# Modulation passes of the first layer: rows of silu(c) in their own slots, loaded by halves, and passes issued at a set rate into the neighbourhood attention

## The chip, the cores and the metric

The kernel runs on one core of a Trainium2 chip. The metric is device time in microseconds of one execution. Before the change it is 1731.88 us, the median of three runs (1730.83, 1731.88 and 1736.24).

The engines are PE (TensorE; PEld is its weight load), DVE (VectorE), ACT (ScalarE), POOL (GpSimd) and SP (SyncE, which here only issues DMAs). Each takes its instructions in order.

## The reference, cut to what matters

One step of a two-layer trunk over 512 latent and 128 context tokens of width 1024, all in float32. Each layer has a modulated norm, a mixer and a gated convolutional feed-forward network. The modulation of a layer is six vectors of width 1024, for two conditioning vectors, `c` (latent tokens) and `c_ctx` (context tokens):

```python
mod = (jax.nn.silu(cvec) @ w + bias).reshape(-1, 1, 6 * D_MODEL)
sh1, sc1, g1, sh2, sc2, g2 = jnp.split(mod, 6, axis=-1)
h = rms_norm(x, norm_mix_g) * (1.0 + sc1) + sh1
x = x + g1 * mixer(h)
x = x + g2 * conv_ffn(rms_norm(x, norm_ffn_g) * (1.0 + sc2) + sh2)
```

The first layer's mixer has two head groups side by side: neighbourhood attention (eight heads, an 8x16 window of the grid and all context keys) and a bidirectional gated linear attention (GLA, four heads, decays from a low-rank gate). The second layer's mixer is grouped-query attention.

## The kernel before, in words

Tokens lie along the free dimension (640 columns, in two halves of 320), features along the partitions. Weights come by SP's DMAs in tiles of 512 KB (`ws`), and ACT and DVE (in the first layer's mixer every second time POOL) split them into a rounded and a remaining part (`wh`, `wl`, lines 111 and 112). A product takes three matmuls for each block of 128 features (line 153).

Stages, each with a pool of its own: `begin` (first norm and modulation), `mix0` (the first layer's mixer, `layer0`, to about 450 us), `ffn0`, `mix1`, `ffn1`.

**The modulation.** Two vectors of the first layer (0 and 1) are made by matmuls in `begin`. The other ten are made on DVE by `modulations` (line 298). `crow` holds `c` and `c_ctx` in a row; a DMA spreads 512 values of it over all partitions and ACT takes the silu (lines 305, 306). Then, for each vector, `ada_wt` gives eight blocks of 128 output features by 1024 inputs, in halves of 512. A step of the generator loads one half block (256 KB, `wa`, three buffers, line 313) and makes two passes over it, for the two conditioning vectors: a product with the row that also sums along the row (line 316, 128x512, with an accumulator read that follows it). So a vector takes 16 steps and 32 passes. The mixer makes vectors 2 to 4 of the first layer (48 steps); `ffn0` makes the other seven (112 steps, one after each evacuation of a product).

**The order.** The framework lists the instructions of each engine by priority in a simulated schedule; priority follows the order in which the program issues them, except where `high_priority` moves a block ahead. `issue_after(x)` holds the instructions of a block that are on the engine of `x` behind `x` in that engine's order; it says nothing of other engines.

**The first layer's mixer.** `layer0` makes keys and queries of the GLA, the low-rank gate, then a class `Fill` holds generators of products (`queue`: value, output-gate, and query and key projections of the attention, some 208 steps of matmuls) that other code draws from by `fill.some(n)`. Its list `aside` holds the generator of the modulation. One step of it is drawn before the gates (line 672). The gates (lines 724 to 747) are four passes over matmul, minimum, Abs, Exp, Ln and a scan along the tokens. Then follow pieces in the order `a0 s0 a1 o0 q0 s1 o1`:

- `a` (`gla_scores`): seven levels of decayed scores; each level makes two factors on DVE (lines 840 to 843, 847), ACT (Exp) and POOL (line 846), and small matmuls (line 860); six level blocks are masked (line 865). At each of six places two steps of the modulation are drawn (`SLEV`), at one more four (`SOFF`).
- `s` (`gla_states`): states of the GLA. Before it, `fill.some(0, 99)` draws all steps that are left.
- `o` (`gla_out`): its outputs. `q` puts the attention's first query and key projection ahead in the filling.

Then comes the neighbourhood attention: 20 units (for each of four head pairs two pairs of query blocks with two heads each, and one context unit) in a software pipeline of stages scores, exps, gather, values, norm and turn, whose `high_priority(offset=AHEAD)` puts them 300 places ahead. Between stages `fill.some(RNA)` draws 1.8 steps of filling. DVE adds the bias (line 1062), takes the maximum (1023) and normalises (1037); PE transposes (1070) and multiplies by the values (1089). The tiles with the transposed weights have the tag `napx` (four buffers), and the four rows of silu(c) in `mix0` use these same buffers.

## Time and profile before

| what | value |
|---|---|
| median of three runs | 1731.88 us |
| profiled execution, its own time | 1732.08 us |
| its span, first to last instruction | 1730.3 us |
| mean granted TensorE clock | 0.97 |
| busy PE, DVE, ACT, POOL | 1640.0, 1280.7, 720.9, 206.5 us |
| chain that ended last | PE 78%, DVE 15%, DMA 3%, ACT 2%, issue 2% |
| matmuls of line 153 in that chain | 66% of the span |
| L316 passes, all 320 in the run | 120.4 + 113.2 us |

"Busy" is time with an instruction running. PE's is pipelined, so full busy time is not its peak rate. The chain is followed back from the last instruction, at each step to what released it. In a group of instructions, "idle before" is the time the engine stood still just before them and what ended it. The granted clock is a share of 2.4 GHz; the other level is 1.2 GHz.

### The profile page before, as it was taken

The page shows a single profiled execution, that of the slowest core. Times are in us where ns is not written, and L with a number is a line of the kernel's source. Part 1 is how long each engine was busy: PE and PEld are TensorE (multiplying, and loading weights), DVE is VectorE, ACT ScalarE, POOL GpSimd, SP SyncE. Part 2 cuts the span into 40 slices and gives each one's busy share as a digit, 9 for nine tenths or more (in the row PEclk, how much of TensorE's full clock was granted, in tenths as well). Part 3 has the DMA queues.
Part 4 walks back from the last instruction along what each step waited for, and adds up shares of the span by engine and source line. Part 5 has one row for each costly group of instructions (what it writes and reads, how often), then busy time and mean ns, then how long its engine had stood idle before and what let it go on. Part 6 is the DMA issues. An engine that isn't in the chain of part 4 may idle for free.

```text
span 1730.3 us, 33463 instructions
## 1 busy us (share of the span) xinstructions
PE 1640.0 (95%) x13142; PEld 1565.2 (90%) x13142; DVE 1280.7 (74%) x2877; ACT 720.9 (42%) x1599; POOL 206.5 (12%) x475
## 2 busy tenths in 40 slices
PE   7978798989999999999999999899999999999997
PEld 6867787878999999999998888789999999999997
DVE  5899955775899989996656987996776644663664
ACT  4443255453533313322335566665453322331342
POOL 2134441210200000000003310100100000000001
PEclk8988889999999999999998999999999999999998
DMA  8624323322255455444232200120222222222222
GB/s 317 204 86 133 108 90 97 101 88 92 81 165 164 152 165 183 151 149 128 70 122 87 68 20 13 42 63 20 80 66 82 74 74 73 74 69 91 72 66 71
DMA packets 68014, 175.22 MB, mean 101 GB/s; under 512 B 7920, under 2 KB 9744, under 8 KB 66832
## 3 DMA queue, kind: packets, MB, share of 16 engines
q1 hardware_dynamic: 67024, 171.48, 30.7%
q8 instruction: 103, 1.69, 0.4%
q0 software_dynamic: 832, 1.60, 0.3%
q14 instruction: 55, 0.45, 0.1%
HBM read 165.71 MB, written 7.34 MB: 100 GB/s over the span
## 4 chain that ended last, share of the span: by engine, by line
PE 78%; DVE 15%; DMA 3%; ACT 2%; issue 2%; SPq 0%; POOL 0%; ACTq 0%; DVEq 0%; POOLq 0%
PE mm L153 66%; DVE junk L316 2%; PE gpo L1297 2%; DVE wa L316 2%; PE gpt L1285 1%; DVE wl L112 1%; PE gs L1276 1%; DMA wa<-in_ada_wt_dram 1%; DVE mx L1023 1%; PE gs L1277 1%; PE napo L1089 1%; PE ss L410 1%; DVE eb L847 1%; DMA x<-in_xT_dram 0%; DVE q L613 0%
## 5 line engine op out<-in xcount | busy, mean ns | idle before, releaser
L153 PE MATMUL mm<-hh,wl 128*128 128x320 f32 x2080 | 652.6, 316 | 5.3 <-DVE x L488 1.9
L153 PE MATMUL mm<-hl,wh 128*128 128x320 f32 x2080 | 648.3, 312 | 0.6 <-DVE hl L456 0.6
L153 PE MATMUL mm<-hh,wh 128*128 128x320 f32 x2080 | 641.9, 312 | 0.0
L111 ACT CAST wh<-ws 128x512 fp32r<-128x512 f32 x376 | 228.8, 615 | 447.8 <-PE mm L153 420.5
L153 PEld LDWEIGHTS mm<-hh,wl 128*128 128x128 f32 x2080 | 394.5, 190 | 15.8 <-issue 5.5
L153 PEld LDWEIGHTS mm<-hl,wh 128*128 128x128 f32 x2080 | 395.2, 190 | 3.0 <-issue 1.2
L153 PEld LDWEIGHTS mm<-hh,wh 128*128 128x128 f32 x2080 | 393.4, 190 | 0.4
L112 DVE TENSOR_TENSOR wl<-ws,wh 128x512 fp32r<-128x512 f32 x348 | 242.2, 699 | 157.4 <-ACT wh L111 156.7
L153 PE MATMUL mm<-glo,wh 128*128 128x320 f32 x704 | 217.6, 310 | 0.0
L153 PE MATMUL mm<-ghi,wh 128*128 128x320 f32 x704 | 217.3, 310 | 0.0
L153 PE MATMUL mm<-ghi,wl 128*128 128x320 f32 x704 | 216.3, 310 | 0.0
L488 DVE SCALAR_TENSOR_TENSOR x<-mm,mod,x 128x192 f32<-128x192 f32 (+2 forms) x240 | 96.6, 435 | 84.1 <-PE mm L153 83.2
L153 PEld LDWEIGHTS mm<-ghi,wl 128*128 128x128 f32 x704 | 132.0, 188 | 0.9 <-issue 0.9
L153 PEld LDWEIGHTS mm<-glo,wh 128*128 128x128 f32 x704 | 132.6, 188 | 0.0
L153 PEld LDWEIGHTS mm<-ghi,wh 128*128 128x128 f32 x704 | 132.4, 188 | 0.1
L316 DVE SCALAR_TENSOR_TENSOR junk<-wa,sb 128x512 f32<-128x512 f32 x160 | 120.4, 757 | 9.4 <-DMA wa<-in_ada_wt_dram 7.0
L316 DVE SCALAR_TENSOR_TENSOR wa<-wa,sb 128x512 f32<-128x512 f32 x160 | 113.2, 714 | 0.2
L522 POOL MEMSET u<- 128x1 f32 x88 | 8.9, 102 | 767.2 <-DVE gate L515 432.5
L525 ACT COPY u<-mm 128x320 f32<-128x320 f32 x88 | 37.8, 431 | 87.6 <-PE mm L153 83.2
L1029 ACT ACTIVATE gp<-gs,mx,rq 128x640 f32<-128x640 f32 x64 | 56.9, 889 | 36.6 <-DVE mx L1025 27.9
L592 PE MATMUL tm<-wl,hh 128*128 128x256 f32 x200 | 61.3, 312 | 8.3 <-ACT v L601 4.0
L528 ACT COPY u<-mm 128x192 f32<-128x192 f32 x88 | 28.4, 322 | 78.8 <-PE mm L153 78.8
(302 smaller groups left out, 2452.7 us busy)
## 6 DMA issues: line engine op xcount, KB each, us to landing
ws<-in_wu_dram SPq DMA_DIRECT2D x88, 512.0 KB
wa<-in_ada_wt_dram SPq DMA_DIRECT2D x160, 256.0 KB
ws<-in_wd_dram SPq DMA_DIRECT2D x32, 448.0 KB
aw<-in_ada_w_dram SPq DMA_DIRECT2D x8, 1024.0 KB
ws<-in_w_ab_dram SPq DMA_DIRECT2D x16, 512.0 KB
ws<-in_wd_dram SPq DMA_DIRECT2D x16, 512.0 KB
x<-in_xT_dram SPq DMA_DIRECT2D x16, 320.0 KB
ws<-in_w_gqa_dram SPq DMA_DIRECT2D x10, 512.0 KB
```

The costliest lines, as they stand in the source:

```text
L111: nc.scalar.copy(hi, src)
L112: eng.tensor_tensor(lo, src, hi, ALU.subtract)
L153: nc.tensor.matmul(ps, x, y[:, s], start=st, stop=sp_)
L316: nc.vector.scalar_tensor_tensor(w if v else junk, w, 1.0, cs[v, j], ALU.mult, ALU.mult, accum_out=acc[:, k, v, j:j + 1])
L410: nc.tensor.matmul(ps[0:rows, c:c + 2], part[:, t], onesd, start=True, stop=True)
L488: nc.vector.scalar_tensor_tensor(x[:, b:e], ps[:, b - HN * h:e - HN * h], gate[:, v, m:m + 1], old[:, b:e], ALU.mult, ALU.add)
L525: nc.scalar.copy(u[:, 1:321], ps)
L528: nc.scalar.copy(u[:, 321:513], ps[:, 0:192])
L592: nc.tensor.matmul(ps, hh[:, s], wlo, start=(k == 0), stop=False)
L847: nc.vector.tensor_tensor(eb[:, 0:NT], eb[:, 0:NT], q[:, 0:NT], ALU.mult)
L1029: nc.scalar.activation(dst, src, AF.Exp, bias=mx[:, i:i + 1], accum_out=sm[:, i:i + 1], **kw)
L1297: last = nc.tensor.matmul(po[64 * f:64 * f + 64, 0:128], vs[t][:, 64 * kv:64 * kv + 64], mates[f]["x"][:, 128 * t:128 * t + 128], start=(t ...
```

## The change: what it does

`Fill.some` loses its second argument. It has a rate, `pace`, in steps of the modulation for each call: 0 to the end of the gates, 0.9 (`PACEG`) in the pieces of the GLA, 0.4 (`PACEN`) in the attention. `beside` draws the steps; each step's DVE instructions are held behind `anchor`, the DVE instruction last noted by the surrounding code (the scans, the mask products, a state's copy, the normalisation). `until` and `all` draw only filling. What is left at the last head pair of the attention is drawn there at once.

`modulations` takes groups of vectors and keeps one half (two rows) of silu(c) at a time. In a group it makes all first halves and then all second halves, or the other way round, beginning with the half that is there. The mixer has the groups (vector 2) and (vectors 3, 4), hence three loads of a half; `ffn0` has seven groups of one vector, hence eight loads of a half, in four buffers. In the mixer the rows have two buffers of their own (tag `sb`). The constant `w2` of the gates moves into a buffer of the mixer, loaded by POOL's DMA queue in the mixer; `adarow` and `kx` move into the stages' pools. The output projection looks its gate `mod[0, 2]` up when it uses it.

```diff
-        def some(self, n, m=0):
-            while m and self.aside:
-                m -= 1
-                if next(self.aside[0], self) is self:
-                    self.aside.pop(0)
+        def beside(self, n):
+
+            while n and self.aside:
+                n -= 1
+                with ExitStack() as behind:
+                    if anchor[0] is not None:
+                        behind.enter_context(tc.issue_after(anchor[0].ins))
+                    if next(self.aside[0], self) is self:
+                        self.aside.pop(0)
+
+        def some(self, n):
+            self.due += self.pace
+            self.beside(int(self.due))
+            self.due -= int(self.due)
+            self.queued(n)
+
+        def queued(self, n):
             self.owed += n
...
     def modulations(todo, room):
 
 
-        cs = {}
-        for v in range(2):
-            for j in range(2):
-                cs[v, j] = b = room()[:, 0:512]
+        cs, at = [], None
+
+        def rows(j):
+            for v in range(2):
+                b = room()[:, 0:512]
                 nc.sync.dma_start(b, a["crow"][:, D * v + 512 * j:D * v + 512 * j + 512].to_broadcast([P, 512]))
                 nc.scalar.activation(b, b, AF.Silu)
...
+        for group in todo:
+            accs = {lg: sp.tile([P, KD, 2, 2], F32, tag="adacc", name="adacc", bufs=3) for lg in group}
+            for j in ((0, 1) if at in (None, 0) else (1, 0)):
+                if j != at:
+                    cs, at = list(rows(j)), j
+                for l, g in group:
+                    n = VECTORS.index((l, g))
+                    for k in range(KD):
+                        w = T("wa", "wa", n=512, bufs=NWA)
+                        nc.sync.dma_start(w, a["ada_wt"][n, k, :, 512 * j:512 * j + 512])
+                        junk = N("junk")[:, 0:512]
+                        for v in range(2):
+                            nc.vector.scalar_tensor_tensor(w if v else junk, w, 1.0, cs[v], ALU.mult, ALU.mult, accum_out=accs[l, g][:, k, v, j:j + 1])
+                        yield
...
-        side = modulations(todo, lambda: T("sb", "sb", n=512, bufs=4)) if todo else iter(())
+        side = modulations([[lg] for lg in todo], lambda: T("sb", "sb", n=512, bufs=4)) if todo else iter(())
...
+        w2 = C("w2")[0:64, 0:512].rearrange("p (d n) -> p d n", d=2)
+        nc.gpsimd.dma_start(w2, a["w2"])
...
-        side = modulations(VECTORS[0:3], lambda: T("sb", "napx", n=512, bufs=4))
+        side = modulations((VECTORS[0:1], VECTORS[1:3]), lambda: T("sb", "sb", n=512, bufs=2))
...
+        fill.pace = PACEG
...
                     fill.until(g_vg)
-                    fill.some(0, 99)
...
+        fill.pace = PACEN
...
-            xs, proj = [], OutProjection(a["w_abo"], 4, mod[0, 2])
+            xs, proj = [], OutProjection(a["w_abo"], 4, lambda: mod[0, 2])
...
+                        fill.beside(999)
                         fill.until(g_late)
...
-            fill.some(RLEV, SLEV)
+            fill.some(RLEV)
...
-        fill.some(ROFF, SOFF)
+        fill.some(ROFF)
...
-SLEV = 2
-SOFF = 4
+PACEG = 0.9
+PACEN = 0.4
```

## Rows read from the trace of the kernel before

**Rows 1.** The page, part 2: busy tenths in 40 equal slices of 43.3 us, one digit a slice, of PE and of DVE.

```profile
PE   7978798989999999999999999899999999999997
DVE  5899955775899989996656987996776644663664
```

**Rows 2.** Windows by stage: begin:end and length, then busy us (and instructions) of each engine, the mean granted TensorE clock as a share of 2.4 GHz, the DMA engines' busy share and GB/s. The first seven windows lie in the first layer, the last one in the second layer's attention.

```profile
54.00:112.00 58.00, 52.32 (x421) 48.46 (x420) 55.22 (x130) 25.06 (x48) 9.71 (x6) 0.94 0.54 178
112.00:222.00 110.00, 84.03 (x1469) 78.23 (x1468) 109.87 (x224) 35.02 (x64) 53.03 (x35) 0.86 0.31 103
222.00:245.00 23.00, 23.00 (x251) 20.97 (x251) 10.14 (x19) 11.78 (x20) 12.35 (x10) 0.83 0.24 76
...
273.00:355.00 82.00, 76.73 (x657) 66.04 (x657) 59.65 (x123) 44.03 (x116) 18.61 (x20) 1.00 0.29 87
355.00:392.00 37.00, 31.12 (x234) 27.05 (x231) 25.47 (x54) 19.45 (x53) 4.77 (x6) 0.91 0.27 87
392.00:460.00 68.00, 65.59 (x447) 60.97 (x446) 44.18 (x107) 28.72 (x56) 7.58 (x27) 0.97 0.29 90
460.00:800.00 340.00, 339.42 (x2315) 339.16 (x2314) 323.00 (x797) 114.49 (x257) 10.19 (x106) 1.00 0.50 158
980.00:1160.00 180.00, 163.50 (x1635) 146.25 (x1635) 157.82 (x441) 116.30 (x277) 20.26 (x14) 0.99 0.13 41
```

**Rows 3.** The same view for two of these windows, of the instructions of line 316 (the modulation passes) alone: DVE busy us and records. Each pass leaves two records, the pass and the read of its accumulator.

```profile
54.00:112.00 58.00, 33.62 (x94) 0.94 0.54 178
112.00:222.00 110.00, 46.19 (x98) 0.86 0.31 103
```

**Rows 4.** The chain of waits, shares by line: first in 54 to 112 us, then in 112 to 222, then in 273 to 392.

```profile
by line: DMA wa<-in_ada_wt_dram 23.4%; DVE junk L316 22.6%; DVE wa L316 17.4%; issue 7.9%; DVE cum L743 6.7%; DVE wl L112 6.1%; DVE gmin L740 4.8%; DVE hl L456 3.3%; DVE cum L745 2.5%; DVE gmin L730 1.4%; DVE v L599 1.2%; DVE acc L865 0.8%;
...
by line: DVE junk L316 20.8%; DVE wa L316 18.1%; DVE eb L847 11.4%; issue 7.3%; DVE eb L843 6.6%; DVE ea L841 6.3%; DVE wl L112 5.4%; DVE ea L840 4.2%; DVE eb L842 4.1%; DVE acc L865 3.7%; DMA ws<-in_w_ab_dram 3.2%; DVE att L895 2.2%; DVE v
...
by line: PE mm L153 30.5%; PE napo L1089 10.0%; DMA bias<-in_na_bias_dram 6.0%; PE napt L1070 4.6%; PE nas L1058 4.1%; DVE hl L112 3.8%; issue 3.4%; DVE mx L1023 3.4%; PE nas L1059 3.1%; DVE kl L699 2.9%; PE grs L984 2.7%; ACT nap L1029 2.5
```

**Rows 5.** Instructions of the gates by source line: min/median/max duration in ns, first and last start in us, shapes.

```profile
L728 PE MATMUL gate<-lr,w x16: 429/429/533, 79.6 to 89.0; 64*128 64x320 f32 x16
...
L730 DVE TENSOR_SCALAR gmin<-gate,b x4: 874/880/882, 82.5 to 91.9; 128x640 f32<-128x640 f32 x4
...
L731 ACT ACTIVATE gabs<-gate,b x4: 775/794/796, 83.4 to 92.8; 128x640 f32<-128x640 f32 x4
...
L733 ACT ACTIVATE gabs<-gabs x4: 737/742/752, 85.5 to 93.7; 128x640 f32<-128x640 f32 x4
L733 ACT ACT_TABLE_LOAD  x1: 1283/1283/1283, 84.2 to 84.2; - x1
...
L740 DVE TENSOR_TENSOR gmin<-gmin,gabs x4: 814/822/825, 96.5 to 104.0; 128x640 f32<-128x640 f32 x4
...
L745 DVE TENSOR_TENSOR_SCAN cum<-gscan,gmin x2: 1478/1480/1482, 104.8 to 110.0; 128x640 f32<-128x640 f32 x2
```

**Rows 6.** Who waited for whom, PE in 112 to 222 us: total us, times, longest us.

```profile
PE lev L860 <- DVE eb L847: 14.2, 6, 5.2
```

**Rows 7.** Timeline around two places in the scores: start us, us, engine, line, operation. A start is the record's; the engine takes the next instruction a little before the last one's record ends.

```profile
119.79 2.22 POOL L112 TENSOR_TENSOR wl<-ws,wh 128x512 fp32r<-128x512 f32 x1 [2.29 <-ACT wh L111]
...
120.80 1.76 DVE L316 SCALAR_TENSOR_TENSOR junk<-wa,sb 128x512 f32<-128x512 f32 x1
...
121.97 1.98 POOL L846 TENSOR_TENSOR ea<-ea,kqg 128x640 f32<-128x640 f32 x1
...
122.49 2.01 DVE L316 SCALAR_TENSOR_TENSOR junk<-wa,sb 128x512 f32<-128x512 f32 x1
...
131.18 0.68 DVE L316 SCALAR_TENSOR_TENSOR wa<-wa,sb 128x512 f32<-128x512 f32 x1
...
131.80 0.68 DVE L316 SCALAR_TENSOR_TENSOR junk<-wa,sb 128x512 f32<-128x512 f32 x1
```

**Rows 8.** Groups of DVE instructions in 112 to 222 us: busy us, mean ns of one, idle before.

```profile
L847 DVE TENSOR_TENSOR eb<-eb,kqg 128x640 f32<-128x640 f32 x13 | 15.4, 1199 | 0.0
L843 DVE TENSOR_TENSOR eb<-cum 128x320 f32<-128x320 f32 x13 | 9.7, 743 | 0.0
...
L840 DVE TENSOR_TENSOR ea<-cum 128x320 f32<-128x320 f32 x14 | 6.7, 478 | 0.0
L865 DVE TENSOR_TENSOR acc<-lev,mask 128x160 f32<-128x160 f32 x22 | 6.0, 310 | 0.0
```

**Rows 9.** Timeline from 45 us: the loads of the rows of c, the first silu of them and the first pass; in brackets the engine's idle time before and what ended it.

```profile
46.17 1.75 SPq L305 DMA_DIRECT2D sb<-in_crow_dram  x4
...
49.47 0.63 ACT L306 ACTIVATE sb<-sb 128x512 f32<-128x512 f32 x1 [1.82 <-DMA sb<-in_crow_dram]
...
54.53 0.69 DVE L316 SCALAR_TENSOR_TENSOR junk<-wa,sb 128x512 f32<-128x512 f32 x1 [2.19 <-DMA sb<-in_crow_dram]
```

**Rows 10.** Who waited for whom, SP's DMA queue in 54 to 222 us: total us, times, longest us.

```profile
SPq L313 <- DVE wa L316: 89.3, 39, 10.4
```

**Rows 11.** The same for PE in 273 to 392 us.

```profile
PE napt L1070 <- DVE nap L1037: 1.5, 2, 1.1
```

**Rows 12.** By source line: the mask products of the scores, and the bias sums of the attention (columns as in Rows 5).

```profile
L865 DVE TENSOR_TENSOR acc<-lev,mask x24: 294/308/316, 111.4 to 221.5; 128x160 f32<-128x160 f32 x24
...
L1062 DVE TENSOR_TENSOR nas<-nas,bias x16: 683/700/700, 273.6 to 385.6; 128x512 f32<-128x512 f32 x16
```

More of the change, by code (lines that the diff above doesn't have):

```diff
@@ L237, in run @@
             pass
+    anchor = [None]
     class Fill:
@@ L243, in __init__ @@
             self.queue, self.aside, self.owed, self.after = [], [], 0.0, None
+            self.pace, self.due = 0, 0.0
         def add(self, gen):
@@ L269, in until @@
             while gen in self.queue:
-                self.some(1)
+                self.queued(1)
         def all(self):
             while self.queue:
-                self.some(1)
+                self.queued(1)
     mod = {}
@@ L286, in spread_modulation @@
             nc.tensor.matmul(ps[j:j + 32, 0:128 * n], siluc[:, r, :], w[:, 128 * n * r:128 * n * (r + 1)], start=(r < 4), stop=(r >= 4))
-        row = sp.tile([P, 256], F32, tag="adarow", name="adarow")[:, 0:128 * n]
+        row = T("adarow", "adarow", n=256, bufs=2)[:, 0:128 * n]
         nc.scalar.copy(row, ps[:, 0:128 * n])
@@ L298, in modulations @@
     def modulations(todo, room):
-        cs = {}
-        for v in range(2):
-            for j in range(2):
-                cs[v, j] = b = room()[:, 0:512]
+        cs, at = [], None
+        def rows(j):
+            for v in range(2):
+                b = room()[:, 0:512]
                 nc.sync.dma_start(b, a["crow"][:, D * v + 512 * j:D * v + 512 * j + 512].to_broadcast([P, 512]))
                 nc.scalar.activation(b, b, AF.Silu)
-        for l, g in todo:
-            n = VECTORS.index((l, g))
-            acc = sp.tile([P, KD, 2, 2], F32, tag="adacc", name="adacc", bufs=2)
-            for k in range(KD):
-                for j in range(2):
-                    w = T("wa", "wa", n=512, bufs=NWA)
-                    nc.sync.dma_start(w, a["ada_wt"][n, k, :, 512 * j:512 * j + 512])
-                    junk = N("junk")[:, 0:512]
-                    for v in range(2):
-                        nc.vector.scalar_tensor_tensor(w if v else junk, w, 1.0, cs[v, j], ALU.mult, ALU.mult, accum_out=acc[:, k, v, j:j + 1])
-                    yield
-            m = new_mod(l, g)
-            for v in range(2):
-                nc.vector.tensor_tensor(m[:, v, :], acc[:, :, v, 0], acc[:, :, v, 1], ALU.add)
-                nc.vector.tensor_tensor(m[:, v, :], m[:, v, :], adab[:, l, g, :], ALU.add)
@@ new lines, in rows @@
+                yield b
+        for group in todo:
[12 more added lines that the diff above has]
+                        yield
+            for l, g in group:
+                m, acc = new_mod(l, g), accs[l, g]
+                for v in range(2):
+                    nc.vector.tensor_tensor(m[:, v, :], acc[:, :, v, 0], acc[:, :, v, 1], ALU.add)
+                    nc.vector.tensor_tensor(m[:, v, :], m[:, v, :], adab[:, l, g, :], ALU.add)
@@ L702, in qk_done @@
             if h == 1:
-                kx = sp.tile([P, CTX], F32, tag="kx", name="kx")
+                kx = T("kx", "kx", n=CTX, bufs=2)
                 nc.scalar.copy(kx, ps[:, 192:320])
@@ L742, in layer0 @@
             if d == 0:
[L743 removed]
+                anchor[0] = nc.vector.tensor_tensor_scan(c, gscan, mins[key], 0.0, ALU.mult, ALU.add)
             else:
[L745 removed]
+                anchor[0] = nc.vector.tensor_tensor_scan(rev(c), gscan, rev(mins[key]), 0.0, ALU.mult, ALU.add)
             cum[key] = c
             fill.some(RG2)
+        fill.pace = PACEG
         with tc.issue_after(last.ins):
@@ L1036, in norm @@
                 w = u["p"][i] if n > 1 else u["p"][i][:, 0:NT]
-                nc.vector.tensor_scalar_mul(w, w, sm[:, i:i + 1])
+                anchor[0] = nc.vector.tensor_scalar_mul(w, w, sm[:, i:i + 1])
         u["exps"], u["norm"] = exps, norm
@@ L1158, in begin @@
             parts, srcs = self.half(self.first, outs)
-            return products(srcs, parts, lambda m, h, ps: residual(xs[m], ps, h, self.gate, m), (("mm", "mm"),), 512)
+            return products(srcs, parts, lambda m, h, ps: residual(xs[m], ps, h, self.gate(), m), (("mm", "mm"),), 512)
         def end(self, outs, xs, olds=None):
@@ L1165, in begin @@
                 run(products(srcs[0:KD - FIN], parts, done, ("ps", ("p1", "p1")), 512))
-            return into_norm(xs, self.gate, begin, srcs, parts, 512, olds)
+            return into_norm(xs, self.gate(), begin, srcs, parts, 512, olds)
     def layer1(xs, rs, mods):
@@ L1318, in layer1 @@
         run(project(1))
-        proj = OutProjection(a["w_gqao"], 0, mod[1, 2])
+        proj = OutProjection(a["w_gqao"], 0, lambda: mod[1, 2])
         ys = []
```

7 lines of the change are left out of this document (2 added, 5 removed).

## The prediction

> **What bounds the kernel now.** I began with the slices of the page: DVE stands at 8 or 9 tenths from 43 to 216 us while PE falls to 7 and 8 tenths, the weakest stretch of the run [rows 1]. The windows by stage say it sharply: from 112 to 222 us DVE is busy 109.87 of 110 us, PE 84.03 at a mean granted clock of 0.86; PE idles 26 us there [rows 2]. The reader should see the other side in the same table: from 460 to 800 us PE is busy 339.42 of 340, so time lost or won before 460 passes straight to the end.
>
> Third, how much of DVE is the modulation passes of line 316: 33.62 us in 54 to 112 (94 records, so 47 passes with their accumulator reads) and 46.19 us in 112 to 222 (98, so 49) [rows 3]. All 48 steps (3 vectors x 16 steps x 2 passes) are over by 222 us. Fourth, the chain: from 54 to 112 it runs through these passes (22.6% and 17.4%) and their loads (23.4%); from 112 to 222 again through them (20.8% and 18.1%) [rows 4]. So the first layer waits for passes whose results are needed only by the output projection and the feed-forward network. In the neighbourhood attention, 273 to 392 us, DVE has 34 us free (59.65 of 82 and 25.47 of 37) and PE is busy 107.85 of 119 [rows 2].
>
> **The change part by part.** What follows is the count of steps. One is drawn before the gates, unpinned. Then each filling call adds 0.9: seven in a0, two in s0, seven in a1, two each in o0, s1, o1, so 22 x 0.9 = 19.8, or 19 steps, 14 of them to the end of a1. The 28 others come at 0.4 a call, so within some 68 calls; five units make 28 calls and the stages lag by up to two units, so that is near the 14th of 20 units.
>
> *A, before the scores (54 to 112).* Of 23.5 steps one is left. What is late next is the gates' own chain. The first gate's matmuls start at 79.6 [rows 5]; two of 0.43 and the minimum of 0.88 end near 81.4. ACT then has four times 0.79 + 0.74, two table loads of 1.28 and the first Ln, priced like an Exp: 9.4, to 90.8. DVE has four differences of 0.82 and four scans of 1.48 left, 9.2, and about 2 us of splits and copies for the filling: 102, against 111.4 now (last scan from 110.0) [rows 5]. I take -9. Bounds: -4, if PE, busy 52.32 of 58, delivers the filling first; -13.6, the share of the loads in the chain alone (23.4% of 58).
>
> *B, scores and states (112 to 222).* Without the 46.19 us DVE holds 63.7. Back come 14 steps, 28 passes. A pass takes 0.615 us from start to start when POOL is quiet (131.18 to 131.80) and on average 46.19/49 = 0.943 here: 17.2 or 26.4 us, sum 80.9 or 90.1, so -29 or -20. PE's 84.03 then lies beside it; at a mean clock of 0.86 a part of it ran at 1.2 of the 2.4 GHz, so it is less at full clock. PE also waits 14.2 us for the second factor of the scores, behind passes on DVE [rows 6], and that shrinks. I take -18, the dearer pass and 2 us for two engines that must alternate. Bounds: -29 and -8.
>
> Why a pass is dear here: at 120.80 one takes 1.69 to the next start, while POOL's split of 119.79 runs to 122.0; the next, at 122.49, lasts 2.01 beside the product that POOL has from 121.97 to 123.95; at 131.18 and 131.80, POOL silent, 0.68 [rows 7]. Others are stretched alike: L843 has a mean of 743 ns where L840, of the same shape, has 478 [rows 8]. The Trainium skill, "SBUF — State Buffer", section "Who interferes with whom", says that a VectorE instruction with two SBUF inputs contends with a GpSimd one that reads SBUF, for the whole instruction, and that issue order decides who blocks. The trace agrees: L865, which has one input in PSUM, keeps 310 ns [rows 8]. By that rule POOL's work blocks whichever such DVE instruction is next, so the waiting is not taken away with the passes. That is a rival below.
>
> *C, 222 to 245.* PE is busy throughout at a clock of 0.83, a part of it at 1.2 GHz, after the idling before; at 2.4 throughout this is 23 x 0.17 = 3.9 us less. I take -2, ends -4 and 0: idle gaps remain.
>
> *D, rows of silu(c) by halves.* Three pairs of rows instead of two, in two slots of their own. Twice in this layer a new half is loaded when the old half's last pass is over: issue, landing, silu, pass. At the start this takes from 46.17 (issue) to 54.53 (first pass), 8.4 us for four rows, with ACT waiting 1.82 for the first landing [rows 9]. In SP's queue the other loads stand behind that issue, which waits for DVE; in ACT's queue two silu of 0.63 and up to two table loads of 1.28 stand before exponentials. Bounds: 0, if the neighbouring work fills the gap, and 16, two full latencies on the path. I take +3, nearer to the hidden end, since ACT has only 35 of 110 us to do in 112 to 222. The weight loads of the passes waited 89.3 us in SP's queue behind passes already [rows 10], so that queue is no new gate.
>
> *E, the neighbourhood attention.* 28 steps are 56 passes of 0.615, 34.4 us. With the 85.12 of 273 to 392 this is 119.5 of 119: no gap is left. The nearest row is the second layer's attention, by the same pipeline: 980 to 1160 with DVE at 157.82/180 = 0.877 and PE at 163.50/180 = 0.908 [rows 2]. At 0.877, 119.5 us need 136, +17. But the attention's stages go ahead in the order, so passes slip behind them, to where DVE has 24 of 68 us free (392 to 460): over 273 to 460, (129.3 + 34.4)/187 = 0.875, just what the second layer bears, +0. Bounds: 0, and +25, if all end with unit 14, near 355: (59.65 + 34.4)/0.877 = 107 for 82. Queued behind each pass on DVE are the bias sum, the maximum, the normalisation; PE waits for these little now (1.5 us for the normalisation) [rows 11]. I take +11, between 0 and 17 and nearer the second layer's crowding.
>
> *The rest.* The feed-forward network of the first layer gets 16 rows where it had 4: 12 x 0.63 = 7.6 us of ACT, busy 114.49 of 340; DVE, busy 323, gets nothing. I take 0, bounds 0 and +5. w2 comes by POOL's queue in the stage itself, before the gates at 79.6, with POOL busy 9.71 of 58: 0, up to +2. The other buffers that move change no instruction. The attention's buffers that held the rows were free by 222, well before its first unit near 273, so giving them back is worth 0.
>
> Sum: -9 -18 -2 +3 +11 = -15. The profiled execution took 1732.08 (span 1730.3, 1.8 around it), 0.2 above the median of 1731.88: 1717.
>
> **The rivals.**
> *More: the passes hide in the attention.* A -9, B -23, C -2, D and E 0: -34, 1698. For it: 58 us of DVE free between 273 and 460, enough for 34. Against it: the free time there is partly the chain's own waiting.
> *The waiting stays.* POOL blocks other two-input work in place of the passes. The waiting is 46.19 - 49 x 0.615 = 16 us; kept whole, 63.7 + 17.2 + 16 = 97 of 110, B = -13, sum -10: 1722. For it: L843 and, with a mean of 1199 ns, L847 are stretched as well [rows 8]. Against it: with DVE no longer full, some of the blocking falls on idle time. The page named under B states the rule behind this.
> *Slower: the attention pays for every pass.* Each pinned pass stands on the in-order DVE in front of a sum, a maximum or a normalisation on which PE's next transposes rest: all 34.4 us lie on the path. A, B, C and D give -26, so +8: 1740. It decides from an attention longer by 26 us. For it: DVE has no time left over in 119. Against it: PE has filling matmuls there (L153 holds 30.5% of the chain [rows 4]) and hardly waits for DVE now.
> *It doesn't do what it says.* The pin only holds a pass behind an instruction of DVE; nothing holds the rest of the scores in front. If the passes still end up in the gaps before the scores, each engine does as before: -2, 1730.
>
> **How the numbers follow.** A measurement tells about 0.3%, 5 us, from no change. Forecast 0.41, more 0.15, waiting stays 0.13, slower 0.19, as before 0.12. Of the forecast and the waiting together 0.06 falls within 0.3%, and of "as before" 0.08, with 0.03 faster and 0.01 slower: faster 0.66, same 0.14, slower 0.20. The bounds of all terms together go further than 1695 to 1740, but they don't fall together; this range takes in the first rival and the last and leaves about 2 in 10 out.
>
> **What would show it.** A right: the last scan ends near 102 and the chain before it has no loads of wa. B: the last L865, now at 221.5, comes near 195, with DVE under 97% busy before it and the clock over 0.86. E: the time from the first L1062 to the last, now 112 us [rows 12], is 5 to 17 us longer, with DVE near 0.9. D: ACT and DVE wait for the crow loads under 5 us in all. Wrong, if the scores don't end 15 us earlier, or if the attention grows by more than 26.

## The result: slower, 1754.34 us, and the profile after

The changed kernel takes 1754.34 us (median of four runs, 1752.76 to 1755.34) against 1731.36 for the kernel before beside it: ratio 1.0131, 95% interval 1.0118 to 1.0143. That is 23 us slower where 15 us faster was forecast. Its profiled span is 1751.0 us against 1730.3, the granted clock 0.963 against 0.970.

The gain forecast up to the end of the scores came, and was lost behind them. Starts in us from the two traces (before: [rows 5, 12] and the first line below):

| milestone | before | after | difference |
|---|---|---|---|
| last scan of the gates | 110.0 | 97.0 | -13.0 |
| last mask product of the scores | 221.5 | 197.1 | -24.4 |
| last copy of a GLA output | 261.1 | 245.1 | -16.0 |
| first bias sum of the attention | 273.6 | 275.9 | +2.3 |
| last bias sum of the attention | 385.6 | 406.9 | +21.3 |

By source line, the copies of the GLA outputs of before, then four milestones of after (count, then min/median/max ns, first and last start):

```profile
L958 ACT COPY got<-go x4: 570/586/587, 246.8 to 261.1; 128x512 f32<-128x512 f32 x4
...
L768 DVE TENSOR_TENSOR_SCAN cum<-gscan,gmin x2: 1478/1480/1481, 90.5 to 97.0; 128x640 f32<-128x640 f32 x2
...
L890 DVE TENSOR_TENSOR acc<-lev,mask x24: 306/311/324, 98.9 to 197.1; 128x160 f32<-128x160 f32 x24
...
L983 ACT COPY got<-go x4: 573/586/590, 226.3 to 245.1; 128x512 f32<-128x512 f32 x4
...
L1087 DVE TENSOR_TENSOR nas<-nas,bias x16: 678/690/700, 275.9 to 406.9; 128x512 f32<-128x512 f32 x16
```

The windows by stage of after (columns as in [rows 2]: PE, PEld, DVE, ACT, POOL busy, granted clock, DMA share, GB/s):

```profile
54.00:112.00 58.00, 52.48 (x445) 48.22 (x444) 37.78 (x53) 30.55 (x56) 20.09 (x11) 1.00 0.25 81
112.00:222.00 110.00, 98.50 (x1665) 89.06 (x1664) 93.60 (x184) 42.45 (x75) 56.33 (x39) 0.91 0.33 104
222.00:245.00 23.00, 19.00 (x140) 16.75 (x138) 9.65 (x24) 11.53 (x23) 7.07 (x7) 0.85 0.26 89
245.00:273.00 28.00, 12.30 (x90) 11.64 (x90) 8.30 (x20) 5.07 (x11) 3.87 (x6) 0.63 0.50 141
275.00:400.00 125.00, 104.77 (x769) 91.82 (x768) 112.58 (x270) 59.45 (x151) 22.84 (x25) 0.84 0.40 126
392.00:460.00 68.00, 67.36 (x479) 61.39 (x478) 38.49 (x81) 26.87 (x61) 1.84 (x13) 1.00 0.24 82
460.00:800.00 340.00, 338.55 (x2301) 336.28 (x2300) 324.09 (x793) 129.37 (x287) 16.66 (x121) 0.99 0.50 161
```

The first two lines are the success: DVE is no longer full (37.78 of 58 for 55.22, 93.60 of 110 for 109.87 [rows 2]) and PE does 98.50 us of work for 84.03. The fourth is a hole that was not there: PE stands 15.7 of 28 us. The fifth is the attention: DVE 0.90 busy, PE 104.77 of 125 at a clock of 0.84. Nothing changes after it: from the start of the last bias sum to the end of the span it takes 1344.7 us before and 1344.1 after. The kernel before in the same 125 us:

```profile
275.00:400.00 125.00, 113.79 (x927) 97.39 (x926) 87.33 (x184) 64.36 (x172) 23.38 (x26) 0.97 0.27 84
```

The hole in the timeline of after (start, us; in brackets idle before and what ended it):

```profile
239.58 4.76 SPq L807 DMA_DIRECT2D vc<-in_na_vc_dram  x1
...
244.44 1.25 SPq L811 DMA_DIRECT2D kc<-in_na_kc_dram  x2
...
245.74 4.09 SPq L333 DMA_DIRECT2D wa<-in_ada_wt_dram  x3
...
246.43 0.31 PE L152 MATMUL mm<-hh,wl 128*128 128x320 f32 x1
...
246.58 0.31 PE L152 MATMUL mm<-hl,wh 128*128 128x320 f32 x1
...
257.86 1.29 ACT L110 CAST kch<-kc 128x512 fp32r<-128x512 f32 x2 [9.41 <-DMA kc<-in_na_kc_dram]
259.31 0.69 DVE L336 SCALAR_TENSOR_TENSOR junk<-wa,sb 128x512 f32<-128x512 f32 x1 [10.95 <-DMA wa<-in_ada_wt_dram]
...
260.12 0.49 DVE L722 TENSOR_TENSOR kl<-mm,kk 64x320 fp32r<-64x320 f32 x1
...
260.76 0.61 PE L152 MATMUL mm<-hh,wl 128*128 128x320 f32 x1 [13.28 <-DVE kl L722]
...
261.96 0.47 PE L152 MATMUL mm<-hl,wh 128*128 128x320 f32 x1
...
262.23 0.47 PE L152 MATMUL mm<-hh,wh 128*128 128x320 f32 x1
```

Read it from the end. PE stands 13.28 us for the keys' split on DVE (L722). DVE has had that split's input since 248.04 + 0.42 (the ACT cast), but a pass (L336) is in front of it in DVE's order and waits 10.95 us for its weights. Those were issued at 245.74, behind the eight value tiles, `vc` and the cached keys, and are used 13.6 us later. Beside this wait stands a second one: ACT waits 9.41 us for the cached keys, issued at 244.44. After the hole PE restarts at the lower level: line 152 starts a matmul every 0.145 us at 246.4 (clock 1.00) and every 0.267 us at 262 (clock 0.50, 1.2 GHz).

The order in SP's queue is new as well. The value tiles (`vw`) and the cached keys (`kc`) in SP's timeline, before and then after:

```profile
237.60 0.90 SPq L787 DMA_DIRECT2D kc<-in_na_kc_dram  x2
...
251.83 13.55 SPq L781 DMA_DIRECT2D vw<-values  x8
```

```profile
228.13 11.35 SPq L805 DMA_DIRECT2D vw<-values  x8
...
244.44 1.25 SPq L811 DMA_DIRECT2D kc<-in_na_kc_dram  x2
```

The program issues these loads in the same order in both kernels; the framework's list put the keys 14 us ahead of the value tiles before the change and 16 us behind them after it. Which part of the change turned the order was not tried alone; e4 below, with the old draws and no pins, has the keys first (244.34 and 258.24), e1, without the steps of the attention, has them last.

### The profile page after: what moved, and what is told of

Read it like the earlier page. It is cut to its first block, busy times and chain, and to the rows that moved or that the text cites. A ratio compares the mean times of both kernels' runs of the same rounds, so it can differ in the third digit from the quotient of the medians.

```text
span 1751.0 us, 33552 instructions
## 1 busy us (share of the span) xinstructions
PE 1652.5 (94%) x13142; PEld 1575.5 (90%) x13142; DVE 1282.4 (73%) x2877; ACT 735.0 (42%) x1617; POOL 209.7 (12%) x475
## 4 chain that ended last, share of the span: by engine, by line
PE 72%; DVE 7%; ACT 1%; issue 1%; POOL 0%; DMA 0%; ACTq 0%; POOLq 0%; DVEq 0%
PE mm L152 63%; PE gpo L1322 2%; PE gpt L1310 1%; PE gs L1301 1%; PE gs L1302 1%; DVE mx L1048 1%; DVE wl L111 1%; PE napo L1114 1%; DVE wa L336 1%; PE ss L431 0%; DVE gp L1062 0%; DVE q L634 0%; PE napt L1095 0%; DVE junk L336 0%; DVE gkl L1253 0%
## 5 line engine op out<-in xcount | busy, mean ns | idle before, releaser
L152 PEld LDWEIGHTS mm<-hh,wl 128*128 128x128 f32 x2080 | 397.5, 191 | 33.8 <-issue 18.9
L336 DVE SCALAR_TENSOR_TENSOR junk<-wa,sb 128x512 f32<-128x512 f32 x160 | 114.7, 722 | 22.0 <-DMA wa<-in_ada_wt_dram 17.1
L336 DVE SCALAR_TENSOR_TENSOR wa<-wa,sb 128x512 f32<-128x512 f32 x160 | 116.9, 738 | 0.3
```

The costliest lines, as they stand in the source:

```text
L152: nc.tensor.matmul(ps, x, y[:, s], start=st, stop=sp_)
L336: nc.vector.scalar_tensor_tensor(w if v else junk, w, 1.0, cs[v], ALU.mult, ALU.mult, accum_out=accs[l, g][:, k, v, j:j + 1])
```

## The experiments

Times are medians, with the ratio and its 95% interval to the kernel before run beside them (1731 to 1732 us each time). "Change" is the changed kernel, 1754.34.

**e1: the change without the 28 steps of the attention.** Loads, passes and the rows' third load are left out; vectors 3 and 4 are summed in part.

```diff
+                        done[0] += 1
+                        if done[0] > limit:
+                            yield
+                            continue
                         w = T("wa", "wa", n=512, bufs=NWA)
...
-        side = modulations((VECTORS[0:1], VECTORS[1:3]), lambda: T("sb", "sb", n=512, bufs=2))
+        side = modulations((VECTORS[0:1], VECTORS[1:3]), lambda: T("sb", "sb", n=512, bufs=2), 20)
```

> The changed kernel with the last 28 steps of the first layer's modulation left out (their loads, passes and the third load of rows; the vectors 3 and 4 are then only partly summed); the 20 steps to the end of the GLA stay as they are. Theory of the queue plus theory of DVE time: all that the change loses comes after the GLA and from these 28 steps, so the gain at the GLA's end, 16 us (last copy of its outputs at 245.1 for 261.1), stays: about 1715. Rival, the new order itself (rows by halves, pins, keys behind the value tiles) costs the time: it stays above 1740.

1729.35, ratio 0.9984 [0.9969, 0.9998]: the steps cost 25 us, yet without them 2 us remain of a forecast gain of 29 (A, B and C), and of the 16 expected. Scores and GLA end as in the change (196.4, 246.7) and the attention is 112.8 us long, as before. Its first bias sum comes only at 267.9, and the chain of waits of e1 says why:

```profile
243.24 12.09 DMA kc<-in_na_kc_dram
```

With the pass gone, the second wait, for the cached keys, is on the path: 12.09 us.

**e2, e3, e5, e6: which wait holds the entry.** e2 lets the first ten calls of the attention draw no step; e3 moves the cached keys' loads ahead of the value tiles' loads in the program; e5 does both; e6 is e1 with e3's edit.

```diff
         def some(self, n):
-            self.due += self.pace
+            if self.skip:
+                self.skip -= 1
+            else:
+                self.due += self.pace
...
         fill.pace = PACEN
+        fill.skip, fill.due = 10, 0.0
```

```diff
+        for c in range(2):
+            kc, x, y = N("kc")[:, 0:512], C("kch", F32R)[:, 0:512], C("kcl", F32R)[:, 0:512]
+            nc.sync.dma_start(kc, a["na_kc"][:, 4 * c:4 * c + 4, :].rearrange("p h t -> p (h t)"))
...
         vw = {}
...
         nc.sync.dma_start(vc, a["na_vc"])
-        for c in range(2):
-            kc, x, y = N("kc")[:, 0:512], C("kch", F32R)[:, 0:512], C("kcl", F32R)[:, 0:512]
-            nc.sync.dma_start(kc, a["na_kc"][:, 4 * c:4 * c + 4, :].rearrange("p h t -> p (h t)"))
```

> The changed kernel, but the first ten filling calls of the attention draw no step (and nothing is owed from the GLA), so that the 21st step's load no longer stands between the value tiles' loads and the first unit. Theory of the queue: the stand of 13.3 us at 247 to 261 goes, at least down to what the wait of ACT for the cached keys leaves of it; 9 to 13 us faster than the change, 1741 to 1745. Theory of DVE time alone: the same 28 steps, a little closer together, so no faster than 1754. Rival of the keys: ACT waits for them until 257.9 anyway, so 3 us at most.

> The changed kernel with the two loads of cached keys issued before the value tiles' loads instead of behind them. Theory of the queue: DVE waits for the pass's own load (10.95 us), not for the keys, so within 3 us of the change, 1751 to 1757. Rival of the keys: ACT's wait of 9.4 us is what holds the stage, so about 9 us faster, 1745.

> Both edits together: the cached keys' loads ahead of the value tiles' loads, and no step for the first ten calls of the attention. Theory of two waits side by side (the first pass's load and the keys, both queued behind the value tiles, each enough to hold the stage): together they give what neither gives alone, 12 to 16 us faster than the change, 1738 to 1743. Rival, the stand has a third cause (the value tiles themselves, or PE's order): no more than the later start alone, 1747.

> The last 28 steps left out as in the first experiment, and the keys' loads ahead. The chain of the first experiment had 12.1 us of the keys' load on it; without it 8 to 12 us less than 1729: 1718 to 1721. The rival with a third cause: 1726 or more. The difference to the run with both edits is the price of the 28 steps in the attention: theory of DVE time 15 to 22 us; rival (the steps are hidden once nothing waits for loads): under 6.

e2: 1747.76 (1.0092 [1.0073, 1.0111]), -6.6, less than expected: its chain of waits has 13.12 us of the keys' load. e3: 1755.03 (1.0131 [1.011, 1.0152]), nothing. e5: 1745.89 (1.0078 [1.0062, 1.0093]), -8.4, less than expected. e6: 1723.01 (0.995 [0.9935, 0.9965]), 6.3 under e1.

The edit of the keys does less than the expectations say. SP's timeline of e6, and the longest piece of its chain of waits:

```profile
227.22 11.13 SPq L820 DMA_DIRECT2D vw<-values  x7
238.43 4.06 SPq L810 DMA_DIRECT2D kc<-in_na_kc_dram  x2
242.58 0.61 SPq L820 DMA_DIRECT2D vw<-values  x1
```

```profile
239.37 14.22 DMA kc<-in_na_kc_dram
```

Seven of the eight value tiles still go first (in e3, e5, e7 and e10 too; in e8 and e15 all eight). The keys are issued 4.2 us earlier than in e1 and land 1.7 us earlier (253.59 for 255.33), so the wait for them is shortened and not gone. e6's first bias sum is at 264.9, e1's at 267.9; where the rest of the 6.3 us comes from was not found. Two waits do stand side by side: shortening the keys' alone wins nothing, taking the pass away leaves the keys' (e1, e2). None of these four runs is without the second.

e5 and e6 differ in the 28 steps (and their third load of rows): 22.9 us. The attention is 130.7 us long in e5, 111.3 in e6. Their windows, e5 and then e6:

```profile
275.00:400.00 125.00, 105.02 (x752) 90.03 (x750) 111.98 (x277) 57.42 (x146) 21.91 (x24) 0.84 0.39 125
```

```profile
275.00:400.00 125.00, 114.51 (x921) 98.26 (x921) 84.90 (x188) 60.04 (x159) 22.42 (x37) 0.96 0.27 84
```

With the steps DVE has 27.1 us more in it, and PE pays twice: 9.5 us more idle, and the work it does is at a mean clock of 0.84, not 0.96. The passes lie on the path: in e5's chain of waits from 266 to 397 us they hold 21.3%, 28 us:

```profile
by line: PE mm L152 16.0%; DVE junk L339 10.7%; DVE wa L339 10.6%; DVE mx L1051 8.2%; issue 6.4%; DVE nap L1065 5.6%; DVE nas L1090 4.9%; DVE hl L111 4.0%; DVE kl L725 3.4%; DVE q L637 3.2%; DVE kk L726 3.0%; DVE wl L111 2.6%; DVE got L1013
```

**e11 to e14: pin, passes or loads.** All on e5. e11 holds no pass of the attention behind a normalisation. e12 keeps the 28 loads and leaves out the passes; e13 keeps both, but passes of 8 elements; e14 keeps full passes over one tile and leaves out the loads. In e12 to e14 vectors 3 and 4 are not the full sums.

```diff
-                    if anchor[0] is not None:
+                    if anchor[0] is not None and self.pace == PACEG:
```

```diff
-                        for v in range(2):
+                        done[0] += 1
+                        for v in range(2 if done[0] <= limit else 0):
```

```diff
+                        done[0] += 1
+                        e = 512 if done[0] <= limit else 8
                         for v in range(2):
-                            nc.vector.scalar_tensor_tensor(w if v else junk, w, 1.0, cs[v], ALU.mult, ALU.mult, accum_out=accs[l, g][:, k, v, j:j + 1])
+                            nc.vector.scalar_tensor_tensor((w if v else junk)[:, 0:e], w[:, 0:e], 1.0, cs[v][:, 0:e], ALU.mult, ALU.mult, accum_out=accs[l, g][:, k, v, j:j + 1])
```

```diff
+                        done[0] += 1
+                        if done[0] <= limit:
+                            w = T("wa", "wa", n=512, bufs=NWA)
+                            nc.sync.dma_start(w, a["ada_wt"][n, k, :, 512 * j:512 * j + 512])
...
```

> Keys first and later start, but the passes of the attention are not held behind a normalisation; in the pieces of the GLA they are held as in the change. Theory (DVE's time is what costs, wherever a pass stands): 1746 within 4, the attention 127 to 132 us long, DVE near 0.9. Rival (a pass costs since it is held in front of a sum or a maximum): the passes move into gaps of DVE, the attention is 118 to 122 us long, 1735 or less.

> Keys first and later start; the 28 steps of the attention issue their weight loads but not their 56 passes (so vectors 3 and 4 are summed in part only); the rows' third load stays. It splits the 22.9 us that the 28 steps cost into loads and passes. Theory (the passes' time on DVE costs): 1723 to 1726, the attention 111 to 114 us long. Rival (the loads in SP's queue or the DMA engines beside the bias and weight loads cost): 1732 or more, the attention over 119 us.

> Keys first and later start; the 28 steps of the attention keep their loads and both passes, held where they were, but a pass goes over 8 elements instead of 512 (vectors 3 and 4 are summed in part only). The loads come at the pace of the attention, which the run with the loads alone did not keep: without a reader they were all issued at its entry. If the passes' time on DVE is the price, 1723 to 1729, the attention 111 to 116 us long. If the loads are the price (SP's queue, where a load waits for the tile of three steps before, in front of the bias loads), 1738 to 1746, the attention over 122 us.

> The counterpart: keys first and later start, the 56 passes of the attention at their full width and place, all over the tile of the last step before, and none of the 28 loads (vectors 3 and 4 are wrong sums for it: their inputs are left out). If the passes' time on DVE is the price, 1740 to 1746, the attention over 124 us. If the loads are the price, 1723 to 1729, the attention 111 to 116 us long. Both prices may add up to more than the 22.9 us, if they overlap.

e11: 1750.02 (1.0109 [1.0092, 1.0126]), 4.1 over e5, and an attention of 136.5 us, longer than expected: the pin is not the price. e12: 1745.29 (1.0075 [1.0056, 1.0093]), a miss and a confounded one: with no reader the loads were issued at the entry, where the chain holds six of them in a row (261.72 to 284.5) in front of a bias load, so the first bias sum came at 277.7 instead of 266.1. e13: 1730.63 (1.0000 [0.9988, 1.0011]); e14: 1739.94 (1.0048 [1.003, 1.0065]). Over e6 that is 7.6 us for the loads at their pace and 16.9 for the passes, 24.5 together against 22.9. The 7.6 are not the loads alone: the short passes still take 9.05 us of DVE from 275 to 400, where e5's take 41.14. So the passes are two thirds of the price or more, the loads one third at most. The windows of e13 and then e14:

```profile
275.00:400.00 125.00, 112.03 (x893) 97.78 (x892) 91.15 (x296) 62.20 (x165) 21.77 (x25) 0.93 0.41 131
```

```profile
275.00:400.00 125.00, 103.50 (x812) 89.12 (x811) 113.97 (x285) 61.67 (x158) 23.12 (x25) 0.92 0.24 72
```

e14 has DVE and PE busy as e5 has them (113.97, 103.50) with the DMA share of 0.24, but a clock of 0.92 for 0.84 and 812 matmuls for 752; e13 has PE nearly as in e6. How e13's 7.6 us arise is not settled: the clock is 0.93, and in SP's queue the loads wait 32.0 us for passes (L345), 14 times, with bias and weight loads behind them.

**e4: halves and slots alone.** The buffers and halves of the change, with the old draws (two and four a place, all that are left before the states) and no pins.

```diff
-                    if anchor[0] is not None:
+                    if False:
...
-            fill.some(RLEV)
+            fill.beside(SLEV)
+            fill.some(RLEV)
...
                     fill.until(g_vg)
+                    fill.beside(99)
```

> Rows by halves in their own slots, w2 and the small buffers as in the change, but the steps drawn as before (2 at each level, 4 at the next place, all that are left before the states) and held behind nothing. Theories of the queue and of DVE time: these parts cost nothing, within 4 us of the kernel before, 1728 to 1736. Rival, the halves: three loads of rows with their silu and table loads cost 5 us or more, 1737 or above.

1738.98 (1.0045 [1.0029, 1.0061]): 7.6 us slower than before, as the rival had it. The last scan is at 98.2, but GLA's outputs end at 275.9 instead of 261.1. The passes come late: 16.93 us of them lie behind 222, where the kernel before has none, and DVE is busy 26.34 of the 28 us from there on. ACT waits 7.8 us for rows. That the halves alone make the passes late is argued: e4 holds all the moved buffers.

**e9, e16, e15, e17: SP's queue or the DMA engines.** e9 puts the keys first in the kernel before. e16 is the change with the value tiles and `vc` in POOL's queue. e15 draws all steps before the attention (8 before the gates, 1.8 a call in the GLA) with the keys first; e17 does so with the value tiles in POOL's queue instead.

```diff
-                nc.sync.dma_start(v, grid[4 * t:4 * t + 4, c0:c0 + 32, :])
+                nc.gpsimd.dma_start(v, grid[4 * t:4 * t + 4, c0:c0 + 32, :])
...
-        nc.sync.dma_start(vc, a["na_vc"])
+        nc.gpsimd.dma_start(vc, a["na_vc"])
```

```diff
-        next(side)
+        for _ in range(8):
+            next(side)
...
-PACEG = 0.9
+PACEG = 1.8
```

> The kernel before the change, with only the loads of the cached keys moved ahead of the value tiles' loads. Theory: the entry of the attention waits for this load with no pass about, as in the experiment without the 28 passes, where the same move gave 6.3 us; there the scores ended 25 us earlier. If the entry waits for it here too, 1725 (-6), with the first bias sum near 268 instead of 273.6. Rival: in the old order the last outputs of the GLA (261) are late enough that the keys are there in time; then 1731 within 2, and the first bias sum stays at 273 to 274.

> The change as it is, except that the eight value tiles and the cached values are loaded through POOL's queue instead of SP's; the order of everything else stays. If the entry of the attention stands still because the weights of its first modulation step and the cached keys lie behind these loads in SP's queue, both come early now: the first bias sum near 264 instead of 275.9 and 1742 to 1746. Rival: it is the DMA engines themselves that are taken, whatever the queue; then the loads land as late as before and 1752 to 1756 stays.

> Keys first, 8 steps before the gates, and twice the rate in the pieces of the GLA (1.8 a call for 0.9), so that all 48 steps are over before the attention; rows by halves as in the change. It keeps a part of the gain before the scores and pays nothing in the attention. Theory: the 39 steps in the GLA give 1.8 DVE us a step as they did before the change, so its outputs end some 5 to 9 us later than in the experiment with 8 early steps (243.4), near 250, and the attention is 112 us long: 1722 to 1730. Rival: the passes are issued too late and stand at the entry before the keys' splits, as in the experiment with the rows alone: 1735 or more.

> 8 steps before the gates, 1.8 a call in the pieces of the GLA, and the value tiles by POOL's queue (the cached keys where the change has them). In the run of the same rates with the value tiles in SP's queue the first bias sum came at 304, behind a weight load of 13 us. If the queue made that, the first bias sum comes near 285 and the time falls by 15 to 22 us: 1744 to 1751. Rival (the passes themselves stand late, not their loads): 1758 or more.

e9: 1732.14 (1.0002 [0.9992, 1.0013]): nothing changes, and nothing could: the kernel before has the keys ahead of the value tiles in SP's queue already (e9: 235.42 and 249.65). e16: 1743.19 (1.0069 [1.0044, 1.0094]), 11.2 under the change, first bias sum at 264.0, both as expected. Its SP queue, and the first piece of its chain of waits from 240 us on:

```profile
236.63 0.33 SPq L333 DMA_DIRECT2D wa<-in_ada_wt_dram  x1
238.46 0.99 SPq L811 DMA_DIRECT2D kc<-in_na_kc_dram  x2
239.69 1.54 SPq L333 DMA_DIRECT2D wa<-in_ada_wt_dram  x2
```

```profile
238.46 10.24 DMA kc<-in_na_kc_dram
```

The weights are issued 9 us earlier than in the change, the keys 6. A load of `wa` now lands 4.5 us after its issue (median from 220 to 275), the keys still take 10.6 and the tiles in POOL's queue 9.4. The place in SP's queue was worth 11.2 us of the whole time; the keys' load is still what the entry waits for, and why it takes 10 to 14 us in these runs was not tried.

e15: 1766.19 (1.0198 [1.0172, 1.0223]), the largest miss. Its GLA outputs end at 262.0, not near 250. The attention is 113 us long, as expected, but begins at 304.1. Its chain of waits:

```profile
265.51 1.14 SPq L813
266.74 13.14 DMA wa<-in_ada_wt_dram
279.91 0.71 DVE junk L336 x2
...
285.67 0.41 ACT kk L722
```

The last passes stand at the entry, their weights behind the value tiles (L813); the keys, first in the program, are issued at 280.64. e17: 1755.22 (1.0148 [1.0118, 1.0178]), 11 less and first bias sum at 296.0, between its theory and its rival. The two also differ in the keys' place in the program. Taking the value tiles out of SP's queue thus gives back about 11 of the 35 us that e15 lies over the kernel before. The rest is not the passes' own time: e17's chain still holds three weight loads in front of late passes.

```profile
246.25 8.00 DMA wa<-in_ada_wt_dram
...
256.49 12.99 DMA wa<-in_ada_wt_dram
...
271.72 3.44 DMA wa<-in_ada_wt_dram
```

**e7, e10, e8, e18: a better version.** e7 is e5 with 8 steps drawn before the gates, e10 with 16. e8 has the keys first, the later start, 8 early steps, a rate of 2.0 in the last GLA pieces and 0.25 in the attention, the rest behind it. e18 is e7 with the value tiles in POOL's queue in place of the keys first.

```diff
-        next(side)
+        for _ in range(8):
+            next(side)
```

```diff
             for i, p in enumerate(ORDER):
+                fill.pace = PACEG if i < 3 else 2.0
                 piece(p[0], int(p[1]))
...
+            fill.beside(999)
...
-PACEN = 0.4
+PACEN = 0.25
```

> Both edits, and eight steps (the first half block row of vector 2) drawn before the gates instead of one; the attention is left with 21 steps. In the change DVE is idle 24 of 67 us from 45 to 112, so they fit. Theory of DVE time: 7 steps fewer in the attention at 0.6 to 0.7 us each, 4 to 5 us less than both edits alone. Rival, the gates come later by what the steps take (7 x 1.23 = 8.6): 4 us more.

> Keys first, later start, and 16 steps drawn before the gates instead of 8 or one, so some 13 are left for the attention. Theory: a step costs 0.8 us in the attention and little before the gates until PE's filling there runs behind; the 8 steps before gave 8.0, so 8 more give 4 to 8: 1730 to 1734. Rival: the gates now wait for the passes as they did before the change (last scan near 108 instead of 101.5), which gives it back: 1738 or more.

> Keys ahead, eight steps before the gates, 0.9 a call in a0, s0, a1, 2.0 in o0, s1, o1, then 0.25 in the attention from its eleventh call and the rest behind the attention, beside the output projection, where DVE has 27 of 60 us free. Theory of DVE time: some 15 steps are left in the attention, so 1718 + 15 x 0.65 = 1728, a little faster than the kernel before. Rival: passes beside the output projection hold its weight splits, 1735 or more.

> 8 steps before the gates, later start in the attention, and the value tiles by POOL's queue in place of the keys first. The run with the keys first took 1737.9, 6.9 over the kernel before, with the GLA's outputs ended at 243.4 and the first bias sum at 262.3. By the queue theory the first bias sum comes 2 to 4 us earlier still, and the attention is as long (125): 1734 to 1737. Rival: POOL, which makes a part of the splits and copies there, is held up by issuing the loads: 1740 or more.

e7: 1737.91 (1.0041 [1.0027, 1.0055]), 8.0 under e5, more than expected. e10: 1740.15 (1.0051 [1.0036, 1.0067]): eight more early steps delay the last scan from 101.5 to 106.3 and the scores to 205.0, and give nothing, as the rival had it. e8: 1752.94 (1.0125 [1.0106, 1.0143]), a miss: its attention is 121.3 us long, but the dense passes brought the entry's waits back. Waits of e8 from 235 to 290 us (total, times, longest):

```profile
ACT sb L324 <- DMA sb<-in_crow_dram: 18.4, 2, 17.9
DVE junk L339 <- DMA wa<-in_ada_wt_dram: 16.1, 2, 8.1
```

e18: 1734.34 (1.0015 [1.0004, 1.0026]), the best version that computes everything. The time is as expected, the first bias sum (262.1) no earlier than e7's 262.3. It takes back 20 of the 23 us and does not beat the kernel before.

## Why the prediction was wrong

The direction fell; half of the chain behind it held. The step that failed most is D's "no new gate", the entry of the attention: from the last copy of a GLA output to the first bias sum it takes 30.8 us where it took 12.5, +18.3, for which the sum had only D's +3, meant for the rows. By the milestones, in us:

| stretch | forecast | measured |
|---|---|---|
| to the last mask product (A, B) | -27 | -24.4 |
| to the last GLA copy (C) | -2 | +8.4 |
| to the first bias sum (D) | +3 | +18.3 |
| to the last bias sum (E) | +11 | +19.0 |
| sum | -15 | +21.3 |

In medians, and adding up by construction: e6, which pays no step in the attention, is 8.4 us under before; the 28 steps add 22.9 (e5); the change's order and early start at the entry add 8.4 more. e6 itself still has 20.9 us from the last GLA copy to the first bias sum.

**A and B: right as a sum.** A was -9 and came as -13.0; B was -18 and came as -11.4, inside its bounds but nearer to the -13 of "The waiting stays". That the two add up so well is partly luck. The gates begin at 72.7 instead of 79.6, and only two passes (1.01 us of line 336) are left in 54 to 112. A and B together were -27 and came as -24.4; the forecast of 195 for the last mask product was 197.1. The dear pass was the right choice: 30.82 us for 32 passes in 112 to 222 is 0.963, forecast 0.943. The wait of [rows 6] shrinks from 14.2 us to 2.9.

**C: failed in sign.** It said -2. From the last mask product to the last copy of a GLA output it takes 48.0 us where it took 39.6. Two windows of after:

```profile
197.00:205.00 8.00, 7.90 (x32) 5.79 (x33) 6.96 (x17) 1.63 (x3) 2.72 (x2) 0.50 0.40 121
...
225.00:235.00 10.00, 7.37 (x44) 6.27 (x44) 1.71 (x5) 3.68 (x10) 1.69 (x2) 0.66 0.28 95
```

PE stands more there (43.90 of 48 us busy in all; before, 39.37 of 40) and has the lower level twice. Another 6 us go between GLA's outputs and the first bias sum even with the value tiles out of SP's queue (18.9 us in e16, 12.5 before), with the keys' load of 10.24 us in e16's chain. What the scores gain is thus 24 us at their end and 9 to 10 at the attention. C counted on a higher clock; the mean is 0.81 from 197 to 245 (0.89 from 221 to 261 before), and why it falls there was not tried.

**D: "so that queue is no new gate" failed.** [rows 10] were of the scores, where these waits cost nothing. Past the end of a1 the same queue holds the value tiles and the cached keys, and D named neither; nor did it allow for the framework putting them in another order. The entry paid 11.2 us for the place behind the value tiles (e16). The rows' own latency was +3; e4, which has the rows and all moved buffers in the old order, measures 7.6; in the change ACT waits 7.1 us for the row loads and DVE 4.3 for the silu (source view of line 321, after), over the 5 given as the sign:

```profile
  DMA sb<-in_crow_dram: 7.1, 2
...
  DVE junk L336: 4.3, 2
```

**E: mis-sized, +11 for 19.0 (22.9 in medians of e5 and e6).** Its bounds, 0 and +25, held it. Three parts of its working failed. The pass was taken at 0.615 us; in 275 to 400 it takes 39.77/52 = 0.765. The loads were taken at nothing, and cost up to 7.6 (e13). And "passes slip behind them" to 392 to 460 did not happen: no record of line 336 lies past 400, since the rest is drawn at the last head pair. DVE near 0.9 was right (112.58 of 125), the growth of 5 to 17 us was 19.0. What was not in the sum is PE's side, a mean clock of 0.84 for 0.97. DVE's share alone does not make it: e14, with DVE and PE as busy, has 0.92.

**The rest: right.** 460 to 800 has PE at 338.55 [rows 2], ACT at 129.37 instead of 114.49, twice the 7.6 us forecast and at no cost that shows.

**The rivals.** "More" is out. "The waiting stays" is half true: L872 (L847 before) still takes 1177 ns where it took 1199 [rows 8], passes 0.963, with POOL at 56.33 us; but DVE had room for it. The Trainium skill, "SBUF — State Buffer", section "Who interferes with whom", has the rule for it: a VectorE instruction with at most one SBUF input, outside the two-port modes, does not contend with GpSimd. The trace agrees: L890, with one input in PSUM, keeps 311 ns here too. "Slower: the attention pays for every pass" was nearest in time (1740), though its attention should have grown by 34.4 and the measured price is two thirds of that; its mechanism is half right: passes lie on the path (28 us of e5's chain), but not for the pin, since e11 without it is no faster. Its sum took -26 for all the rest, which is -8.4 in e6. "Doesn't do what it says" is out: 28 steps moved. The range's upper end, 1740, was too low because it let no second term fail beside E.

## What to carry to other kernels

When work moves past a stage boundary, list what else is issued at the boundary on every in-order queue it crosses, its loads first, and read the order from the trace, since the framework may list the same program anew: a pass that waits 11 us for its weights holds all that stands behind it on its engine. Of two waits that end within 2 us of each other, shortening the one that ends first shows nothing, and taking away the other shows less than its length. Price a step in its new place at that place's own duration, with its loads, and count what a standing PE does to the clock behind it.

## What the runs showed of the hardware

Loads of the value tiles move slowly: from 236 to 244 us, with them in SP's queue, the DMA engines are busy 0.26 to 0.36 at 98 to 127 GB/s, where 20 to 25 us of the same trace have 420 GB/s. In e16, in POOL's queue, the eight are issued by 0.68 us of POOL each and land 9.4 us later. The 512 KB of cached keys are there only 10 to 14 us after their issue (13.4 in the change, 14.22 in e6, 10.24 in e16). And a standstill of 13.28 us of PE is followed by matmuls at 0.267 us from start to start instead of 0.145.
